# Slots and banks given out by the longest free time, and gathered rows transposed as fp32r

## The chip, the cores and the metric

The kernel runs on one core of one Trainium2 chip. The metric is the device time of one execution in microseconds (us); lower is better. The core has five engines that run side by side: TensorE (PE in the views, PEld for its weight loads), VectorE (DVE), ScalarE (ACT), GpSimd (POOL) and SyncE (SP), which here only issues DMAs. Each engine takes its own instructions in the order in which they stand in the program; engines wait for one another, and for DMAs, on semaphores.

## What is computed

Two decoder layers over 512 tokens of width 1024, in float32. Each layer mixes the tokens with two kinds of attention, normalizes, sends every token to 2 of 16 experts, and normalizes again. Cut to what matters here:

```python
def reference(x, w_in, ..., exp_w_gate, exp_w_up, exp_w_down, ln2_g, ln2_b):
    for l in range(DEPTH):                                   # DEPTH = 2
        mix = token_mixer(x, w_in[l], ...)                   # sparse and stick-breaking attention
        x = layer_norm(DN_ALPHA * x + mix, ln1_g[l], ln1_b[l])
        ffn = grouped_moe(x, w_router, router_bias, exp_w_gate[l], exp_w_up[l], exp_w_down[l])
        x = layer_norm(DN_ALPHA * x + ffn, ln2_g[l], ln2_b[l])
    return x

def grouped_moe(...):
    # scores, the best group of 4 experts, the 2 best experts in it, weights that sum to 1
    for e in range(N_EXPERTS):                               # 16 experts, D_EXPERT = 512
        h = jax.nn.silu(xf @ exp_w_gate[e]) * (xf @ exp_w_up[e])
        y = y + combine[:, e:e + 1] * (h @ exp_w_down[e])
```

## The kernel before

**Products.** A float32 product is made of three products of a faster type, fp32r (float32 bits, read in a reduced way): each operand is split into a high part (a cast, on ScalarE) and a low part (the difference, on VectorE), and TensorE adds low by high, high by low and high by high into one PSUM bank (`mm3`). So every weight tile that arrives by DMA (512 KB, one slot) goes through one ScalarE cast and one VectorE subtraction, and each of the two writes a slot of its own before TensorE reads it.

**The recorder and its plan.** The kernel body doesn't issue instructions; it records operations on named buffers. A planner in Python (`Recorder.plan`) then walks through them with an estimated duration for each, orders them on every engine, and gives every buffer a place: one of 48 SBUF slots `s` of 4 KB in each of the 128 partitions, of 56 small ones `m`, of 8 `t` or the one `k`, or one of 4 PSUM banks `p` and 4 banks `a`. `room` says when enough places are free for an operation, `take` picks which ones. At run time a buffer in a place waits, through semaphores, until the last reader of the buffer that had the place before is done; this is the only thing that the choice of a place can alter at run time. In the views a tile is named by its place, so `s` stands for any of the 48 slots, `p` and `a` for banks; `ident` is the identity matrix for transposes, `x1d` and `zd` are arrays in DRAM.

**Loads.** All weights and inputs are loaded by SyncE (line 526), one DMA after another in the planned order, each into a slot from the same 48. A load waits at the head of this queue until its slot is free.

**One expert.** `moe` runs over the 16 experts. For experts 1 to 15 `gather` (line 1179, GpSimd) fetches up to 128 token rows from `x1d` by an index list into a slot `xg`; `transpose_tile` turns it by 8 transposes of 128x128 on TensorE (line 445) into a bank `a`, and the split into high and low parts follows. Expert 0 takes its rows from two banks that a product with one-hot rows filled. Then come gate, up and down products (line 447), and 4 more transposes of the hidden activations (`turn` in `down`). `add_rows` (line 1184, GpSimd) adds the result rows into `zd` by an indirect DMA, called scatter-add below; it reads its slot until it has landed. The last expert's rows are added on TensorE instead. Its up product runs in two halves of 256 columns.

**The overflow block.** An expert that gets more than 128 rows is finished by `overflow` (lines 1199 to 1234), a branch on all engines behind the gather of the last expert's work. For these inputs the branch is not taken. Its buffers, five slots `s` among them, are taken from the planner like others and count as free again after it. At run time the skipped branch still brings up the semaphores that its DMAs would have brought up, on GpSimd's queue (names that begin with DMASW; DMAHW are SyncE's queue).

**Closing LayerNorm.** The rows of `zd` are loaded back into slots, multiplied by the identity into banks `p` (`p<-s,ident`) together with the last expert's rows, and normalized on VectorE and ScalarE.

The lines of `take` that set the choice before: `s.sort()` orders the free places of a kind by the time at which they became free, and the index is the largest whose time is not after now.

Of the kernel before, what the change touches and what calls it, by code (L numbers as in the profile page):

```python
# [11 lines left out]
F = mybir.dt.float32  # L12
FR = mybir.dt.float32r
# [9 lines left out]
P = 128  # L23
S = 512
D = 1024
# [28 lines left out]
class View:  # L54
# [19 lines left out]
    def real(self):  # L74
        x = self.buf.tile
        for f, a, k in self.chain:
            x = getattr(x, f)(*a, **k)
        return x
# [13 lines left out]
class Recorder:  # L92
# [82 lines left out]
    def plan(self):  # L175
# [93 lines left out]
        def take(o, t):  # L269
            for b in o.allocs:  # L270
                s = slots[b.kind]
                s.sort()
                i = max((j for j in range(len(s)) if s[j][0] <= t + 1e-9), default=0)
                b.slot = s.pop(i)[1]
                g = b.group
                if g is not None:
                    if live[g] >= self.QUOTA[g]:
                        heapq.heappop(glive[g])
                        live[g] -= 1
                    live[g] += 1  # L280
                    turn[g].pop()
# [3 lines left out]
        while done < len(self.ops):  # L285
            best = None
            for e in engs:
# [3 lines left out]
                t = free[e] if ready[e] else (pend[e][0][0] if pend[e] else None)  # L291
                if t is not None and (best is None or t < best[0]):
                    best = (t, e)
            if barrier and not any(p.prio < barrier[0].prio for e in engs for p in [x[3] for x in pend[e]] + [x[2] for x in ready[e]] if p.prio < barrier[0].prio):
                o = barrier.pop()
                t = max([o.ready] + [free[x] for x in engs if x != "SP"])
# [3 lines left out]
                t = w  # L300
                e = "ALL"
            else:
                if best is None:
                    self.explain(blocked, slots, live)
                t, e = best
# [3 lines left out]
                o = None  # L309
                if e == "ACT" and table is not None:  # L310
                    keep = [x for x in ready[e] if x[2].table in (None, table)]
                    if keep:
                        x = min(keep)
                        if x[0] < ready[e][0][0] + 400:
                            ready[e].remove(x)
                            heapq.heapify(ready[e])
                            o = x[2]
                if o is None:
                    o = heapq.heappop(ready[e])[2]
# [100 lines left out]
class Chip:  # L420
# [13 lines left out]
    def mm(self, out, terms, start, stop, transpose=None, also=()):  # L434
        dt = {F: 4, FR: 1, BF: 1}
        n = self.n(out)
        if transpose is not None:
            dur = 0.11
        else:
            dur = sum(max(dt[x.dtype if not isinstance(x, View) else x.ap.dtype] * n, 256) / 2400 + 0.004 for _, x in terms)  # L440

        def fn():
            o = real(out)
            if transpose is not None:
                self.nc.tensor.transpose(o, real(transpose[0]), transpose[1])  # L445
            for i, (w, x) in enumerate(terms):
                self.nc.tensor.matmul(o, real(w), real(x), start=start and i == 0, stop=stop and i == len(terms) - 1)  # L447
        reads = [x for t in terms for x in t] + ([transpose[0]] if transpose else [])
        o = self.r.add("PE", dur, fn, [out], reads, allocs=also)
        o.cols = sum(n * w.shape[0] / P for w, _ in terms) + n * (transpose is not None)  # L450
        o.cnt = sum(2 if (x.ap.dtype if isinstance(x, View) else x.dtype) == F else 1 for _, x in terms) + (transpose is not None)
        return o
# [91 lines left out]
def build(tc, x0, xT0, w_idx, w_main, w_br, w_out, w_exp, bgate, idxg, idxb,  # L544
          ln1g, ln1b, ln2g, ln2b, wrt, rbias, ln1c, hconst, tab0, out):
    nc = tc.nc
    with ExitStack() as ctx:
# [17 lines left out]
        C = Chip(R)  # L565


        ident = const.tile([P, P], F, name="ident")
        make_identity(nc, ident)
        identb = const.tile([P, P], BF, name="identb")  # L570
        nc.vector.tensor_copy(identb, ident)
        jp = const.tile([P, P], I32, name="jp")
# [28 lines left out]
        def s4(shape, dtype=F, group=None, reserve=0):  # L601
            return R.buf("s", shape, dtype, group, reserve)
# [10 lines left out]
        wr = const.tile([P, KD, NE], F, name="wr")  # L613
        rb = const.tile([P, NE], F, name="rb")
        lnc = const.tile([P, DEPTH, 2, KD], F, name="lnc")
        onesf = const.tile([P, P], F, name="onesf")
        nc.vector.memset(onesf, 1.0)
        loaded = []
        bias_t = const.tile([P, 256 + 384 + 512], BF, name="bias")
# [56 lines left out]
            for n in range(2):  # L676
                C.stt(dst[:, half(n)], dst[:, half(n)], rstd, b[:, half(n)], OP.mult, OP.add)

        def transpose_tile(src, dst_of):
            for hb in range(2):  # L680
                ps = bank("a")
                for k in range(4):
                    c = (hb * 4 + k) * P
                    C.tr(ps[:, k * P:(k + 1) * P], src[:, c:c + P], ident)
                dst_of(hb, ps)

        def proj_tok(l, xT, c, done, before=None):
# [489 lines left out]
        def gather(dst, idx, also, skip):  # L1177
            kw = dict(bounds_check=S - 1, oob_is_err=False) if skip else {}
            R.add("POOL", 1.04, lambda: nc.gpsimd.indirect_dma_start(  # L1179
                out=real(dst), out_offset=None, in_=x1d, in_offset=IOA(ap=real(idx), axis=0), **kw),  # L1180
                [dst], [idx], rtok=[f"x1{t}" for t in range(NT)], nbytes=P * (2048 if skip else 4096), allocs=also)
# [58 lines left out]
        def moe(l, tb, gl, mci, loads, xacc, until, routed):  # L1240
            def prep(e):
                xh, xl = s4([P, KD, P], FR, "xh"), s4([P, KD, P], FR, "xh")

                def dst(hb, ps):
                    ks = slice(hb * 4, hb * 4 + 4)
                    C.split(xh[:, ks, :], xl[:, ks, :], ps.rearrange("p (k t) -> p k t", k=4))
                if e == 0:
                    xg = s4([P, D], group="xg")
                    C.copy(xg[:, half(0)], xacc[0])
                    C.v("tensor_copy", xg[:, half(1)], xacc[1])  # L1250
                    transpose_tile(xg, dst)
                    return xh, xl
                xg = s4([P, D], group="xg")
                last = e == NE - 1
                gather(xg, gl[:, 0:1] if last else tb[:, e, 0:1], [xh, xl], not last)
                transpose_tile(xg, dst)
                return xh, xl

            def weights(e, i):
# [330 lines left out]
```

## Time and profile before

| | |
|---|---|
| median of 3 runs | 1536.97 us (1535.93 to 1539.32) |
| the profiled execution | 1539.54 us |
| its span (first to last instruction) | 1537.7 us |
| TensorE, VectorE, ScalarE busy | 1475.2, 1249.5, 896.6 us |
| granted TensorE clock, mean | 0.983 |
| moved by DMA | 308.52 MB, mean 201 GB/s |

The span falls into attention of layer 0 (to about 360 us), merge, first LayerNorm and router (to about 460), experts (to about 747) and the second LayerNorm, and the same for layer 1, which ends with the output.

How to read the lines below. A line of the timeline has the start, the length, engine, source line, operation, tiles written and read, shape and count of a run of like instructions, and in brackets the idle time before it with what ended it. A line of the waits has who waited for whom: total, times and the longest. A line of the stretches has the stretch, its length, busy time of PE, PEld, DVE, ACT and POOL, the granted clock, the DMA engines' share and GB/s. A group has its count, its busy time, the mean ns of one, and the idle time before. Matmuls overlap: the mean ns of one includes its latency, and the rate is read from many in a row.

### The profile page before, as it was taken

Reading aid. Unit: us, or ns where it says so; the run is one execution under the profiler, and the core shown is the slowest. Engines: PE = TensorE matmul, PEld = TensorE weight load, DVE = VectorE, ACT = ScalarE, POOL = GpSimd, SP = SyncE. Lnnn points to the kernel's source line nnn. Section 1 sums busy time; section 2 is a strip of 40 time slices with the busy share of each in tenths; the row PEclk is TensorE's granted clock in tenths of the full one; section 3 lists DMA queues with packets and bytes.
Section 4 is the critical chain, followed back from the end, with each engine's and each line's share of the span. In section 5 each row is a group of like instructions: output and inputs, shape, how many; then the busy total and the mean of one; then the engine's idle time right before and its main releaser. Section 6 shows DMA issues by size and latency. Waiting matters only on the chain. (4 is left out here: it accounts for less than half of the span.)

```text
span 1537.7 us, 21018 instructions
## 1 busy us (share of the span) xinstructions
PE 1475.2 (96%) x7188; PEld 1178.9 (77%) x7188; DVE 1249.5 (81%) x2301; ACT 896.6 (58%) x1459; POOL 142.4 (9%) x127
## 2 busy tenths in 40 slices
PE   8999999999989999999799999999999899999985
PEld 7877777777867878888588777777778578888874
DVE  5699996777587989999765999867766789999975
ACT  4335543675146878888623455446831478888873
POOL 0000000000031131210010000000001212112110
PEclk9999999999999999999999999999999899999998
DMA  6221112117888989999712221221287889999962
GB/s 217 71 91 57 68 56 89 63 42 288 302 280 297 337 309 348 341 334 333 237 61 69 83 61 50 82 83 55 70 306 279 302 307 351 341 352 339 351 216 108
DMA packets 91265, 308.52 MB, mean 201 GB/s; under 512 B 15439, under 2 KB 15567, under 8 KB 91152
## 3 DMA queue, kind: packets, MB, share of 16 engines
q1 hardware_dynamic: 82000, 290.69, 53.5%
q0 software_dynamic: 9152, 16.43, 4.5%
q8 instruction: 58, 0.95, 0.2%
q14 instruction: 55, 0.45, 0.1%
HBM read 293.80 MB, written 28.46 MB: 210 GB/s over the span
## 5 line engine op out<-in xcount | busy, mean ns | idle before, releaser
L447 PE MATMUL p<-s,s 128*128 128x512 f32 (+1 forms) x5192 | 1268.1, 398 | 28.1 <-DVE s L495 25.7
L447 PEld LDWEIGHTS p<-s,s 128*128 128x128 f32 x5192 | 952.9, 191 | 234.9 <-DVE s L495 25.5
L495 DVE TENSOR_TENSOR s<-s,s 128x1024 fp32r<-128x1024 f32 (+2 forms) x526 | 612.1, 1195 | 152.4 <-ACT s L484 112.3
L484 ACT CAST s<-s 128x1024 fp32r<-128x1024 f32 (+2 forms) x526 | 518.2, 1029 | 226.6 <-PE p L447 141.6
L495 DVE TENSOR_TENSOR s<-a,s 128x256 fp32r<-128x256 f32 (+3 forms) x386 | 169.5, 479 | 36.5 <-ACT s L484 32.7
L484 ACT CAST s<-a 128x256 fp32r<-128x256 f32 (+2 forms) x354 | 127.1, 414 | 109.8 <-PE a L445 103.7
L445 PE MATMUL a<-ident,s 128*128 128x128 f32 x888 | 134.0, 277 | 13.5 <-DMA s<-x1d,m 6.4
L445 PEld LDWEIGHTS a<-ident,s 128*128 128x128 f32 x888 | 106.7, 142 | 44.9 <-issue 11.5
L523 POOL TENSOR_TENSOR m<-m,nhalf 128x1 f32<-128x1 f32 x24 | 17.8, 741 | 891.0 <-DVE m L495 881.6
L480 ACT ACTIVATE s<-a 128x512 f32<-128x512 f32 (+3 forms) x156 | 61.9, 450 | 46.0 <-PE a L447 27.5
L484 ACT COPY s<-a 64x512 f32<-64x512 f32 (+1 forms) x48 | 27.8, 583 | 96.7 <-PE a L445 45.3
L1184 POOL DMA_INDIRECT zd<-s,m x30 | 61.1, 2035 | 199.8 <-ACT s L487 167.4
L487 ACT ACTIVATE s<-p,m 128x512 f32<-128x512 f32 (+1 forms) x64 | 44.1, 689 | 53.5 <-PE p L447 50.6
L1179 POOL DMA_INDIRECT s<-x1d,m x30 | 43.6, 1452 | 267.9 <-PE p L447 220.2
L464 PE MATMUL a<-s,s 64*128 64x384 f32 (+3 forms) x456 | 67.4, 351 | 0.0
L447 PEld LDWEIGHTS a<-s,s 128*128 128x128 f32 x360 | 57.0, 188 | 9.2 <-issue 2.2
L447 PE MATMUL a<-s,s 128*128 128x324 f32 (+4 forms) x360 | 62.2, 321 | 1.5 <-DVE s L495 1.3
L464 PEld LDWEIGHTS a<-s,s 64*128 64x128 f32 x456 | 41.3, 185 | 27.6 <-issue 20.4
L495 DVE MAX8 m<-s 128x8 f32<-128x256 f32 (+2 forms) x96 | 53.4, 556 | 1.8
L495 DVE MATCH_REPLACE8 s<-m,s 128x256 f32<-128x256 f32 (+2 forms) x96 | 52.0, 542 | 0.0
L495 DVE TENSOR_TENSOR_SCAN s<-s 128x128 f32<-128x128 f32 (+3 forms) x64 | 51.0, 812 | 0.1
L484 ACT CAST s<-p 128x512 fp32r<-128x512 f32 x48 | 27.9, 588 | 38.5 <-DVE p L495 22.7
(107 smaller groups left out, 632.4 us busy)
## 6 DMA issues: line engine op xcount, KB each, us to landing
s<-in_w_exp SPq DMA_DIRECT2D x384, 512.0 KB
s<-in_w_main SPq DMA_DIRECT2D x79, 512.0 KB
s<-in_w_br SPq DMA_DIRECT2D x16, 512.0 KB
s<-in_w_out SPq DMA_DIRECT2D x16, 512.0 KB
x1d<-s SPq DMA_DIRECT2D x8, 512.0 KB
zd<-s SPq DMA_DIRECT2D x8, 512.0 KB
s<-zd SPq DMA_DIRECT2D x8, 512.0 KB
s<-in_w_idx SPq DMA_DIRECT2D x8, 324.0 KB
```

Of the source, the lines that this page charges most:

```text
L445: self.nc.tensor.transpose(o, real(transpose[0]), transpose[1])
L447: self.nc.tensor.matmul(o, real(w), real(x), start=start and i == 0, stop=stop and i == len(terms) - 1)
L464: self.nc.tensor.matmul(real(o), real(t[i][0]), real(t[i][1]), start=i == 0, stop=stop and i == len(t) - 1)
L480: self.nc.scalar.activation(real(out), real(src), func, bias=real(bias), scale=real(scale), **kw)
L484: return self.r.add("ACT", 0.1 + self.psum(out, src) + self.n(out) * 0.833e-3, lambda: self.nc.scalar.copy(real(out), real(src)), [out], [ ...
L487: return self.r.add("ACT", 0.2 + self.n(out) * 0.833e-3, lambda: self.nc.scalar.mul(real(out), real(src), real(c)), [out], [src, c])
L495: getattr(self.nc.vector, method)(real(out), *[real(a) for a in args], **{k: real(x) for k, x in kw.items()}, **({} if accum is None else ...
L523: return self.r.add("POOL", 0.47, lambda: self.nc.gpsimd.tensor_tensor(real(out), real(a), e, OP.pow), [out], [a])
L1179: R.add("POOL", 1.04, lambda: nc.gpsimd.indirect_dma_start(out=real(dst), out_offset=None, in_=x1d, in_offset=IOA(ap=real(idx), axis=0), * ...
L1184: rows = R.add("POOL", 1.04, lambda: nc.gpsimd.indirect_dma_start(out=zd, out_offset=IOA(ap=real(idx), axis=0), in_=real(src), in_offset=None,
```

## The change

Two edits. In `take`, the place is no longer the one freed last but, for every kind except `m`, index 0 of the sorted list: the one that has been free longest. And the gathered rows are held and transposed as fp32r: `xg` is an fp32r tile (the gather writes it through a float32 view), `transpose_tile` gets the matrix to transpose by as an argument, and the output bank is viewed in that matrix's type. The identity is now an fp32r tile `identr`, copied by VectorE from a float32 one at the start; the other transposes read it through a float32 view. The float32 identity is built in the tile `onesf`, which is set to ones afterwards.

```diff
@@ take @@
-                i = max((j for j in range(len(s)) if s[j][0] <= t + 1e-9), default=0)
+                i = max((j for j in range(len(s)) if s[j][0] <= t + 1e-9), default=0) if b.kind == "m" else 0
@@ tr @@
-                self.nc.tensor.transpose(o, real(transpose[0]), transpose[1])
+                self.nc.tensor.transpose(o.bitcast(transpose[1].dtype), real(transpose[0]), transpose[1])
@@ constants @@
-        ident = const.tile([P, P], F, name="ident")
-        make_identity(nc, ident)
+        onesf = const.tile([P, P], F, name="onesf")
+        make_identity(nc, onesf)
+        identr = const.tile([P, P], FR, name="identr")
+        nc.vector.tensor_copy(identr, onesf)
+        ident = identr.bitcast(F)
...
-        onesf = const.tile([P, P], F, name="onesf")
         nc.vector.memset(onesf, 1.0)
@@ transpose_tile @@
-        def transpose_tile(src, dst_of):
+        def transpose_tile(src, dst_of, by=ident):
...
-                    C.tr(ps[:, k * P:(k + 1) * P], src[:, c:c + P], ident)
+                    C.tr(ps[:, k * P:(k + 1) * P], src[:, c:c + P], by)
@@ prep, experts 1 to 15 @@
-                xg = s4([P, D], group="xg")
+                xg = s4([P, D], FR, group="xg")
...
-                gather(xg, gl[:, 0:1] if last else tb[:, e, 0:1], [xh, xl], not last)
-                transpose_tile(xg, dst)
+                gather(xg.bitcast(F), gl[:, 0:1] if last else tb[:, e, 0:1], [xh, xl], not last)
+                transpose_tile(xg, dst, identr)
```

The number of free places at any time does not depend on which is picked, so the order of the operations stays nearly the same; what changes nearly everywhere is the slot numbers and with them the waits. Below, a name like s45_14898 is slot 45 and the buffer's number; the brackets list the semaphores that the instruction waits on.

VectorE behind the overflow block of layer 1, in the last expert: the low parts of its last weights (128x1024), and the product's other half taken up (128x256). Before:

```order
L495 TENSOR_TENSOR s25_14889<-s47_14572,s31_14766 128x1024 [waits DMAHW3_49,Activation_49]
L495 TENSOR_TENSOR s45_14898<-s16_14589,s35_14891 128x1024 [waits DMASW0_49,DVE_49,DMAHW4_49,PE_49,Activation_49]
L495 TENSOR_TENSOR s27_14912<-s43_14603,s33_14896 128x1024 [waits DMAHW5_49,PE_49,Activation_49]
L495 TENSOR_TENSOR s43_14930<-s22_14618,s16_14917 128x1024 [waits DMASW1_49,DMAHW6_49,DVE_49,Activation_49]
L495 TENSOR_TENSOR s42_14907<-s42_14907,p1_14900 128x256 [waits PE_49]
```

Now:

```order
L495 TENSOR_TENSOR s47_14890<-s20_14573,s38_14767 128x1024 [waits DMAHW3_49,DVE_49,Activation_49]
L495 TENSOR_TENSOR s11_14899<-s2_14590,s4_14892 128x1024 [waits DMAHW4_49,PE_49,Activation_49]
L495 TENSOR_TENSOR s17_14913<-s30_14604,s13_14897 128x1024 [waits DMAHW5_49,PE_49,Activation_49]
L495 TENSOR_TENSOR s15_14931<-s8_14619,s5_14918 128x1024 [waits DMAHW6_49,PE_49,Activation_49]
L495 TENSOR_TENSOR s16_14908<-s16_14908,p1_14901 128x256 [waits PE_49]
```

No row moved; the second and fourth had slots of the overflow block (s45, whose weights the block would load) or tied to GpSimd's queue, and now have not.

The same place in layer 0. Before:

```order
L495 TENSOR_TENSOR s44_7401<-s25_7107,s41_7393 128x1024 [waits DMASW4_49,DMAHW6_49,PE_49,Activation_49]
L495 TENSOR_TENSOR s43_7417<-s2_7232,s45_7399 128x648 [waits DMASW7_49,DMASW3_49,DMAHW5_49,DVE_49,Activation_49]
L495 TENSOR_TENSOR s35_7432<-s47_7127,s10_7415 128x1024 [waits DMASW3_49,DMAHW7_49,PE_49,Activation_49]
L495 TENSOR_TENSOR s46_7407<-s46_7407,p3_7403 128x256 [waits PE_49]
L495 TENSOR_TENSOR s42_7454<-s0_7234,s25_7428 128x648 [waits DMAHW6_49,Activation_49]
```

Now:

```order
L495 TENSOR_TENSOR s33_7398<-s29_7112,s22_7390 128x1024 [waits DMAHW5_49,PE_49,Activation_49]
L495 TENSOR_TENSOR s1_7412<-s39_7125,s36_7396 128x1024 [waits DVE_49,DMAHW6_49,PE_49,Activation_49]
L495 TENSOR_TENSOR s3_7427<-s43_7136,s20_7417 128x1024 [waits DVE_49,DMAHW7_49,PE_49,Activation_49]
L495 TENSOR_TENSOR s5_7407<-s5_7407,p1_7400 128x256 [waits PE_49]
L495 TENSOR_TENSOR s26_7449<-s46_7256,s4_7425 128x648 [waits DMAHW5_49,Activation_49]
```

A weight split of the next layer (128x648, second row before) moved behind one of the last expert's; the three waits on GpSimd's semaphores are gone from these rows.

ScalarE in layer 0, among the first experts, 12 rows behind the last one that writes s23_5337, which a scatter-add then reads; weights are cast to their high parts. Before:

```order
L484 CAST s47_5447<-s31_4884 128x1024 [waits DMASW7_49,DMASW5_49]
L484 CAST s44_5456<-s43_4899 128x1024 [waits DMASW3_49,DVE_49]
L484 CAST s2_5465<-s25_4912 128x1024 [waits PE_49]
L484 CAST s23_5477<-s29_4929 128x1024 [waits DMASW2_49]
L484 CAST s4_5484<-s26_5155 128x1024 [waits DMAHW3_49,DVE_49,PE_49]
```

Now the same scatter-add reads s34_5332, and its slot goes to VectorE's row in the middle here, the low part of the weight before that of s29_4929:

```order
L495 TENSOR_TENSOR s30_5460<-s37_4899,s28_5446 128x1024 [waits Activation_49]
L495 TENSOR_TENSOR s1_5472<-s42_4911,s43_5454 128x1024 [waits DMASW3_49,DVE_49,Activation_49]
L495 TENSOR_TENSOR s34_5485<-s7_4925,s12_5464 128x1024 [waits DMASW2_49,Activation_49]
L495 TENSOR_TENSOR s23_5414<-s23_5414,p1_5431 128x512 [waits PE_49]
L495 TENSOR_TENSOR s4_5504<-s47_4955,s33_5474 128x1024 [waits Activation_49]
```

So the wait for the scatter-add moved from ScalarE to VectorE, and one weight forward.

## The prediction

> **What bounds the kernel now.** I read the page first (its busy times, the slices and the granted clock), then the waits of TensorE, then the stretches, and last the timeline at each place where TensorE stood still.
>
> ```profile
> PE 1475.2 (96%) x7188; PEld 1178.9 (77%) x7188; DVE 1249.5 (81%) x2301; ACT 896.6 (58%) x1459; POOL 142.4 (9%) x127
> ...
> PEclk9999999999999999999999999999999899999998
> ...
> zd<-s,m POOLq DMA_INDIRECT x30, 9.2
> ```
> ```profile
> PE p L447 <- DVE s L495: 28.2, 15, 6.7
> PE a L445 <- DMA s<-x1d,m: 6.4, 5, 2.6
> ```
> ```profile
> 40.00:360.00 320.00, 318.77 (x1629) 249.61 (x1629) 263.18 (x628) 164.07 (x362) 1.96 (x3) 1.00 0.21 69
> ...
> 480.00:720.00 240.00, 236.72 (x1107) 195.51 (x1106) 217.10 (x212) 197.15 (x237) 45.40 (x25) 0.99 0.98 340
> ```
>
> TensorE is the bound: 1475.2 of 1537.7 us. In the attention stretch of layer 0 it is busy 318.77 of 320 us, so slot numbers there have nothing to hide or to give. Its waits on VectorE add up to 28.2 us in 15 waits; these are few and large, and the change can reach only some. In the experts' stretch TensorE is busy 236.72 of 240 us beside a DMA share of 0.98: two resources nearly full at once.
>
> **The transposes.** Each expert from 1 to 15 transposes 8 blocks of gathered rows, in one run with 4 blocks of the hidden activations:
>
> ```profile
> 603.57 1.47 PE L445 MATMUL a<-ident,s 128*128 128x128 f32 x12
> 604.80 16.62 PE L447 MATMUL p<-s,s 128*128 128x512 f32 x72
> 621.26 1.47 PE L445 MATMUL a<-ident,s 128*128 128x128 f32 x12
> ```
> ```profile
> 752.68 1.88 PE L447 MATMUL p<-s,ident 128*128 128x512 f32 x4
> ```
> ```profile
> L447 PE MATMUL p<-s,ident 128*128 128x512 f32 x24 | 11.4, 596 | 2.5 <-DVE s L495 2.5
> ```
>
> The 12 transposes occupy 1.47 us; less the last one's latency of 0.27 they start every 0.109 us. The fp32r products (72 in 16.62 us, the last 0.39) start every 0.229 us for 512 columns, a quarter of which is 0.057. The plain f32 products by the identity (4 in 1.88 us, the last 0.59) start every 0.43 us, a quarter of which is 0.107. So a transposing of 128 f32 columns costs what plain f32 costs, and fp32r streams at nearly twice the rate. The kernel already runs 64 fp32r products of 128 columns, in pairs behind a pair of 256 columns:
>
> ```profile
> 134.77 0.57 PE L447 MATMUL a<-s,s 128*128 128x256 f32 x4
> 135.19 0.29 PE L445 MATMUL a<-ident,s 128*128 128x128 f32 x1
> ```
> ```profile
> L447 PE MATMUL a<-s,s 128*128 128x256 f32 x2 | 0.4, 283 | 0.0
> L447 PE MATMUL a<-s,s 128*128 128x128 f32 x2 | 0.3, 248 | 0.0
> ```
>
> The four start within 0.42 us of the next instruction; two halves of 0.229 leave 0.19, or 0.095 for each of 128 columns, the step to another kind included. Upper end: 240 transposes (30 experts by 8) by (0.109 - 0.06) = 11.8 us. With 0.095 it would be 3.4. Lower end: 0, if something else sets the 0.109. I take 10, near the upper end because 0.107 meets 0.109 so closely that streaming must set it, and less than it because the first two gathers of a layer are waited for anyway (6.4 us above). The other 648 transposes keep f32.
>
> The Trainium skill, "TensorE: Matmul & The Clock Gate", section "LDWEIGHTS (loading the stationary operand)", gives a weight load P/1.2 ns, with P the columns; an estimate from it is 107 ns for 128 columns. By that rule the weight loads would set the 0.109 us, fp32r would save nothing, and the sum below would be 10 us smaller. The row of 0.109 agrees with it; the pairs of 128 columns, at 0.095 or less, speak against it.
>
> **The ends of the layers.** After the last gate products stands the overflow block, a branch that is not taken here. Its SBUF tiles count as freed at that moment, so "freed last" hands them to the next weight splits; VectorE then waits on the GpSimd queue's DMA semaphores, which come up only behind the last scatter-add.
>
> ```profile
> 1490.92 2.18 POOL L1184 DMA_INDIRECT zd<-s,m  x1 [7.12 <-ACT s L484]
> ```
> ```profile
> 1498.12 3.68 DVE L495 TENSOR_TENSOR s<-s,s 128x1024 fp32r<-128x1024 f32 x3 [6.45 <-DMA zd<-s,m]
> ```
> ```profile
> 1499.40 3.36 PE L447 MATMUL p<-s,s 128*128 128x256 f32 x14 [5.12 <-DVE s L495]
> 1503.27 2.12 PE L447 MATMUL p<-s,s 128*128 128x256 f32 x15 [0.51 <-DVE s L495]
> ...
> 1512.47 1.88 PE L447 MATMUL p<-s,ident 128*128 128x512 f32 x4
> ```
> ```profile
> 741.33 3.48 PE L447 MATMUL p<-s,s 128*128 128x256 f32 x18 [3.87 <-DVE s L495]
> ...
> 760.60 1.98 PE L447 MATMUL p<-s,ident 128*128 128x512 f32 x4 [2.46 <-DVE s L495]
> ```
> ```profile
> 739.72 1.23 DVE L495 TENSOR_TENSOR s<-s,s 128x1024 fp32r<-128x1024 f32 x1 [3.15 <-DMA zd<-s,m]
> ```
> ```profile
> 740.00:750.00 10.00, 7.29 (x35) 6.12 (x36) 9.31 (x12) 5.59 (x8) 0.00 (x0) 0.83 0.79 268
> ...
> 1490.00:1510.00 20.00, 13.11 (x74) 11.37 (x73) 8.91 (x11) 6.12 (x8) 2.18 (x1) 0.83 0.33 102
> ```
>
> In the changed order the same splits of VectorE name only hardware-queue, TensorE, ScalarE or VectorE semaphores; one ScalarE cast at each end still names a GpSimd one, of a scatter two uses of its slot earlier, a whole expert back. Layer 1: the idle 5.12 us goes, and with it part of the reduced clock behind it (14 products in 3.36 us against 15 in 2.12; 0.83 granted): about 1.3 us more. What is late next is the reload of the scattered rows for the closing LayerNorm: its queue also waits for the last scatter, which lands near 1498, while that LayerNorm's first product runs at 1512.47, or about 1506 afterwards; 8 us are left, enough for four loads. So this end is worth 6 of at most 6.9 (5.12 + 0.51 + 1.3), and nothing hides it: it is the program's tail. Layer 0: TensorE idles 3.87, VectorE 3.15, and the LayerNorm that follows waits for VectorE (2.46 at 760.60). What carries through is therefore VectorE's 3.15; I take 3 (ends 0 and 5.2, which is 3.87 and 1.3 of clock).
>
> **Slots that a scatter-add still reads.** Two stalls in the experts:
>
> ```profile
> 557.30 0.50 PE L447 MATMUL p<-s,s 128*128 128x512 f32 x1 [1.81 <-ACT s L484]
> 558.56 7.73 PE L447 MATMUL p<-s,s 128*128 128x512 f32 x20 [0.76 <-DVE s L495]
> ```
> ```profile
> 556.21 2.94 ACT L484 CAST s<-s 128x1024 fp32r<-128x1024 f32 x3 [6.64 <-DMA zd<-s,m]
> ```
> ```profile
> 540.28 7.45 POOL L1184 DMA_INDIRECT zd<-s,m  x1 [5.03 <-ACT s L487]
> ```
> ```profile
> 540.00:580.00 40.00, 37.43 (x164) 30.37 (x163) 32.46 (x33) 28.63 (x36) 12.06 (x4) 0.91 0.90 310
> ```
> ```profile
> 1258.27 5.89 PE L447 MATMUL p<-s,s 128*128 128x512 f32 x23 [1.91 <-DVE s L495]
> ```
>
> At 557 a cast wants the slot whose scatter-add was issued at 540.28 and held GpSimd for 7.45 us, where others take about 2. It costs 2.57 us of idle time and some 3 more of clock (a granted 0.91 over 40 us is 3.6 us, part of it inside the idle time). The changed order does not free this place: the slot of the same scatter goes to VectorE's split of the weight one before, so the wait stands a little earlier. If that scatter is as late again, the stall stays or grows by 1; if it is not, neither kernel shows it. Ends -1 and +5.6; I take 1. At 1258 the split's new slot has no scatter behind it: 1.91, all of it.
>
> **The rest.** The banks: at 366.72 and 1126.65 TensorE waits 1.82 us for the first of four banks, all in use, before and after; no gain.
>
> ```profile
> 366.72 3.48 PE L447 MATMUL p<-s,s 128*128 128x512 f32 x14 [1.82 <-DVE s L495]
> ```
>
> The loads are queued in the same order. In attention they may run further ahead, which no engine waits for; in the experts the queue is at 0.98. The extra copy of the identity is one 128x128 VectorE copy, like this one, and the first product comes 5 us later behind input loads:
>
> ```profile
> 1.46 0.25 DVE L571 CAST identb<-ident 128x128 bf16<-128x128 f32 x1 [1.46 <-POOL ident masks.py:199]
> ```
>
> Its bounds are 0 and 0.25; I take 0. TensorE's instructions that wait grow by about 250 in number; those satisfied long before cost nothing visible (the 72 products above keep 0.229 with such waits among them). I allow -2 for those that are not, and for the loads: an expert's 12 loads of 0.524 MB take 18.5 us at 340 GB/s against TensorE's period of 17.69 (603.57 to 621.26), so the lead gained in attention shrinks, and faster by 0.39 it shrinks more, 14 times: at worst 5.5 us a layer.
>
> ```profile
> s<-in_w_exp SPq DMA_DIRECT2D x384, 512.0 KB
> ```
> ```profile
> ACT s L484 <- DMA s<-in_w_idx: 2.2, 1, 2.2
> ```
>
> The second row is the only wait for a load among ScalarE's waits from 480 to 740 us, and it is not for an expert's. At the start of layer 1 some VectorE rows and one load change places; VectorE sets the pace there in both orders, so I take 0, with 2 either way.
>
> Sum: 10 + 6 + 3 + 1 + 1.9 - 2 = 20 us. The profiled execution took 1539.5 (span 1537.7 and 1.8 around it), which is 2.6 above the median of 1537.0; the sum would make it 1519.5, and 1517 of the median.
>
> **The rivals.** First, the loads become the bound: share 0.98 speaks for it, that no cast waits for an expert's load speaks against. It takes up to 11 of the 11.8 and leaves the stalls (6 + 3 + 1 + 1.9, less 1 for waits): 1537 - 11 = 1526. Second, fp32r transposes are no faster (half of the change does nothing): 1537 - 20 + 10 = 1527; the quarter of an fp32r product, 57 ns, speaks against. Third, slower: "longest free" in a pool that the experts keep almost empty returns the slots of scatter-adds a set distance behind each scatter, and VectorE or ScalarE then stops in every expert as at 557. One such stop costs up to 5.6 us; it decides from four more stops (22 us), and six would give 1537 - 20 + 34 = 1551. For it speaks that a scatter takes 9.2 us to land and that the changed split at 557 waits earlier; against it, that the slots' distance does not shrink elsewhere. Fourth, both halves cancel against new waits: 1537.
>
> **How the numbers follow.** Forecast 0.6, loads 0.11, no gain from fp32r 0.14, slower 0.09, no change 0.06. A measurement tells about 0.2%, 3 us. Faster 0.85, same 0.06, slower 0.09. The forecast's own range is 1506 (11.8 + 6.9 + 5.2 + 5.6 + 1.9 = 31.4) to 1525; taking in the two rivals of 1526 and 1527, with a profile's noise on them, the range is 1506 to 1529.
>
> **What would show it.** Right: runs of transposes per expert of about 1.1 us for 12, a period near 17.3; no wait of VectorE on scatters around 736 and 1492 and no idle TensorE of 4 to 5 us there; the stall at 1258 gone. Wrong: 1.47 us for 12 as now; casts that wait for expert loads near the end of a layer; waits on scatters in many experts with clock drops behind them.

## The result, and the profile after

| | before | after |
|---|---|---|
| median, runs side by side | 1538.14 us (1535.93 to 1541.99, 4 runs) | 1513.52 us (1512.39 to 1515.85, 4 runs) |
| ratio | | 0.9839, interval 0.9815 to 0.9863 |
| span of the profiled execution | 1537.7 us | 1511.4 us |
| TensorE busy | 1475.2 us | 1460.1 us |

The change makes the kernel 24.6 us faster, 1.6%. Measured once more in a later group it took 17.8 us off (0.9885, interval 0.9863 to 0.9907; experiment 4). What makes the two gains differ by 6.8 us is not known. All medians and ratios leave out two executions far slower than the rest, of 8018 us (`fr_only`) and 2081 us (the kernel before, experiment 5).

The page of the profile after, its first busy line, and then the longest waits of TensorE (who waits for whom, total, times, longest):

```profile
PE 1460.1 (97%) x7188; PEld 1168.7 (77%) x7188; DVE 1242.7 (82%) x2302; ACT 890.7 (59%) x1459; POOL 141.4 (9%) x127
```
```profile
PE p L447 <- DVE s L495: 20.4, 13, 6.7
PE a L445 <- DMA s<-x1d,m: 7.7, 4, 5.2
```

Waits on VectorE fell from 28.2 to 20.4 us; the wait for gathered rows grew from 6.4 to 7.7.

The timeline of TensorE after, at one expert in the steady run of layer 0, at the end of layer 0, and at the end of layer 1 (the views write f32 for fp32r too; the name `identr` marks the new identity, which the f32 transposes of other tiles read as well):

```profile
592.95 1.23 PE L445 MATMUL a<-identr,s 128*128 128x128 f32 x12
594.01 16.59 PE L447 MATMUL p<-s,s 128*128 128x512 f32 x72
610.44 1.23 PE L445 MATMUL a<-identr,s 128*128 128x128 f32 x12
...
707.20 0.60 PE L445 MATMUL a<-identr,s 128*128 128x128 f32 x4
...
725.96 2.42 PE L447 MATMUL p<-s,s 128*128 128x256 f32 x18 [0.51 <-DVE s L495]
...
736.35 1.88 PE L447 MATMUL p<-s,identr 128*128 128x512 f32 x4
...
746.78 3.78 PE L447 MATMUL p<-s,identr 128*128 128x512 f32 x4 [4.96 <-DVE s L495]
750.35 1.28 PE L445 MATMUL a<-identr,s 128*128 128x128 f32 x8
```
```profile
1458.70 12.54 PE L447 MATMUL p<-s,s 128*128 128x512 f32 x54
...
1477.48 2.06 PE L447 MATMUL p<-s,s 128*128 128x256 f32 x15 [0.52 <-DVE s L495]
...
1486.43 1.88 PE L447 MATMUL p<-s,identr 128*128 128x512 f32 x4
```

An expert's period is 610.44 - 592.95 = 17.49 us, 0.20 less than the 17.69 before. At the layer ends the idle 3.87 us are down to 0.51 and the 5.12 are gone. But the LayerNorm behind layer 0 now stands still for 4.96 us where it stood for 2.46. The same marks in the timeline of before:

```profile
719.22 0.60 PE L445 MATMUL a<-ident,s 128*128 128x128 f32 x4
...
762.42 1.04 PE L445 MATMUL a<-ident,s 128*128 128x128 f32 x8
...
1477.71 12.54 PE L447 MATMUL p<-s,s 128*128 128x512 f32 x54
```

From the last expert's 4 transposes to the LayerNorm's first product by the identity (752.68 and 1512.47 before) the end of layer 0 takes 29.15 us instead of 33.46, 4.3 less, and from its 54 products on the end of layer 1 takes 27.73 instead of 34.76, 7.0 less. From that first product to the first 8 transposes the LayerNorm behind layer 0 takes 14.0 instead of 9.7: 4.3 more.

### The profile page after: what moved, and what is told of

Same layout as the page of the kernel before. It is cut to its first block, busy times and chain, and to the rows that moved or that the text cites. A ratio compares the mean times of both kernels' runs of the same rounds, so it can differ in the third digit from the quotient of the medians.

```text
span 1511.4 us, 20936 instructions
## 1 busy us (share of the span) xinstructions
PE 1460.1 (97%) x7188; PEld 1168.7 (77%) x7188; DVE 1242.7 (82%) x2302; ACT 890.7 (59%) x1459; POOL 141.4 (9%) x127
## 5 line engine op out<-in xcount | busy, mean ns | idle before, releaser
L495 DVE TENSOR_TENSOR s<-s,s 128x1024 fp32r<-128x1024 f32 (+1 forms) x526 | 606.8, 1192 | 84.6 <-ACT s L484 72.0
L484 ACT CAST s<-s 128x1024 fp32r<-128x1024 f32 (+1 forms) x526 | 515.6, 1033 | 67.7 <-PE p L447 28.2
L445 PE MATMUL a<-identr,s 128*128 128x128 f32 x888 | 125.0, 271 | 14.3 <-DMA s<-x1d,m 7.7
L445 PEld LDWEIGHTS a<-identr,s 128*128 128x128 f32 x888 | 102.5, 142 | 44.6 <-issue 15.5
L523 POOL TENSOR_TENSOR m<-m,nhalf 128x1 f32<-128x1 f32 x24 | 17.8, 743 | 877.8 <-DVE m L495 509.5
L1186 POOL DMA_INDIRECT zd<-s,m x30 | 56.0, 1868 | 254.5 <-ACT s L487 205.2
L1181 POOL DMA_INDIRECT s<-x1d,m x30 | 47.5, 1583 | 203.3 <-PE p L447 103.1
```

The lines of the kernel that those rows point to most:

```text
L445: self.nc.tensor.transpose(o.bitcast(transpose[1].dtype), real(transpose[0]), transpose[1])
L484: return self.r.add("ACT", 0.1 + self.psum(out, src) + self.n(out) * 0.833e-3, lambda: self.nc.scalar.copy(real(out), real(src)), [out], [ ...
L495: getattr(self.nc.vector, method)(real(out), *[real(a) for a in args], **{k: real(x) for k, x in kw.items()}, **({} if accum is None else ...
L523: return self.r.add("POOL", 0.47, lambda: self.nc.gpsimd.tensor_tensor(real(out), real(a), e, OP.pow), [out], [a])
L1181: R.add("POOL", 1.04, lambda: nc.gpsimd.indirect_dma_start(out=real(dst), out_offset=None, in_=x1d, in_offset=IOA(ap=real(idx), axis=0), * ...
L1186: rows = R.add("POOL", 1.04, lambda: nc.gpsimd.indirect_dma_start(out=zd, out_offset=IOA(ap=real(idx), axis=0), in_=real(src), in_offset=None,
```

## The experiments

Ten kernels ran, two of them twice, in three groups; each group shares runs of the kernel before on its chip. "New order" is the choice of the place free longest, "old order" that of the place freed last.

### 1. Each half of the change alone

`fr_only` has the fp32r transposes under the old order (all of the diff but its first line); `lru_only` has the new order with the f32 transposes:

```diff
@@ take, lru_only @@
-                i = max((j for j in range(len(s)) if s[j][0] <= t + 1e-9), default=0)
+                i = max((j for j in range(len(s)) if s[j][0] <= t + 1e-9), default=0) if b.kind == "m" else 0
```

> Only the fp32r transposes; places are again given out by the time freed last. Theory: 8 of the 12 transposes of an expert start every 0.084 instead of 0.109 us, 0.2 us an expert, so 240 of them are worth 5 to 6 us and no more; the idle TensorE behind the overflow block (about 4 and 5 us) stays, and VectorE's waits on scatter-adds there with it. About 1532 against 1538. Rival, that the two halves help only together: no difference from the kernel before, within 2 us.

> Only the choice of the place freed longest; transposes in f32 as before. Theory: the changed kernel's gain of 24 us less the 5 to 6 of the transposes, about 18 to 19, so 1519; the waits behind the overflow block are gone in both layers. Rival, that the time went with a slow scatter-add that only the profiled run of the kernel before had: 10 to 12 us of gain, about 1527.

Before 1535.14. `fr_only` 1531.7, ratio 0.9986 (0.9962 to 1.001): inconclusive, between 6 us faster and 2 slower. `lru_only` 1511.82, 23.3 us faster, 0.9847 (0.9818 to 0.9876). So the new order alone gives what the whole change gives, better than the 18 to 19 that I expected, and the fp32r transposes nothing that these runs show. Yet they save TensorE time: `fr_only` has the period of 17.49 too, `lru_only` that of 17.69 (593.64 to 611.33).

```profile
593.64 1.47 PE L445 MATMUL a<-ident,s 128*128 128x128 f32 x12
594.87 16.62 PE L447 MATMUL p<-s,s 128*128 128x512 f32 x72
```

### 2. What in the new order does it: overflow slots, all slots, banks

`mru_spare` keeps the old order, but takes a slot of the skipped overflow block only when no other is free; `lru_s` has the new order for the slots `s` alone, `lru_banks` for the banks `p` and `a` alone.

```diff
@@ take, mru_spare @@
+                if (b.kind, s[i][1]) in spare:
+                    i = max((j for j in range(len(s)) if s[j][0] <= t + 1e-9 and (b.kind, s[j][1]) not in spare), default=i)
+                spare.discard((b.kind, s[i][1]))
@@ plan, where a buffer's place becomes free @@
+                    if o.eng == "ALL" and b.kind == "s":
+                        spare.add((b.kind, b.slot))
@@ take, lru_s and lru_banks: the end of the line, one each @@
+ ... if b.kind != "s" else 0
+ ... if b.kind not in "pa" else 0
```

> The kernel before with one rule more: places are given out by the time freed last, but SBUF slots that the overflow block held are taken only when no other slot is free. Theory: the two waits behind the block were due to these slots alone, so both go: 7 us at the end of layer 1 and 3 to 4 at the end of layer 0, of which the LayerNorm after may take some back; 1528 to 1531. Rival, that the waits there come from any slot tied to a scatter-add: the idle 4 and 5 us stay, 1537 to 1538.

> The place freed longest for SBUF slots alone; PSUM banks by the time freed last; transposes in f32. Theory: the banks do nothing, since TensorE's waits for banks stood where all four were in use, so the time is that of the run with both, within 2 us. Rival: banks freed long ago spare TensorE short waits in every stretch, and 4 us or more of the gain are missing here.

> The kernel before with the new order for the PSUM banks alone; the slots in SBUF still go to the one freed last. Theory (slots carry the change, banks take 1 to 5 us, the difference of the new order for both and for slots alone, 4.8 us between medians and 2 between profiles): 1 to 5 us below the kernel before, and the waits of 3.9 and 5.1 us at the two layer ends stay. Rival (banks alone are worth nothing, they only help once the slots are spread): within 1 us of the kernel before.

| | median | ratio |
|---|---|---|
| `mru_spare` | 1526.41 (before 1535.14) | 0.9936 (0.9913 to 0.996) |
| `lru_s` | 1516.64 (before 1535.14) | 0.9874 (0.9841 to 0.9907) |
| `lru_banks` | 1533.15 (before 1534.7) | 1.0004 (0.998 to 1.0027) |

Timelines of TensorE at the layer ends: `mru_spare` (lines are 6 higher), then `lru_banks`.

```profile
736.00 2.42 PE L453 MATMUL p<-s,s 128*128 128x256 f32 x18 [1.16 <-DVE s L501]
...
1470.69 18.25 PE L453 MATMUL p<-s,s 128*128 128x512 f32 x93
1489.45 2.06 PE L453 MATMUL p<-s,s 128*128 128x256 f32 x15 [0.51 <-DVE s L501]
```
```profile
732.27 4.21 PE L447 MATMUL p<-s,s 128*128 128x256 f32 x18 [4.60 <-DVE s L495]
...
1486.48 3.36 PE L447 MATMUL p<-s,s 128*128 128x256 f32 x14 [5.33 <-DVE s L495]
```

Keeping the overflow block's slots out of the way takes away 2.7 of the 3.87 us at the end of layer 0 and all 5.12 at the end of layer 1, where TensorE runs on without that gap (the 0.51 at 1489.45 was there before too); it is worth 8.7 us, about what was expected. The mechanism in the prediction is shown by this: the slots of a branch that isn't taken carry the semaphores of GpSimd's queue.

The new order for all slots is worth 18.5, so 9.8 more than keeping the overflow block's slots away. That is clear of the noise (every run of `mru_spare` lies above every run of `lru_s`), but where it comes from stays open. The two profiles differ by 7.8 us: 2.8 before the experts of layer 0, 4.1 in those experts, where `mru_spare` has a late scatter-add (experiment 3), and some 1 behind; the first two also differ between profiles of one order.

The banks alone show nothing, between 3 us faster and 4 slower, and the end stalls stay with them, as expected. Slots and banks together (`lru_only`) are 4.8 below slots alone, and all five runs (1510.95 to 1515.06) lie below all four of `lru_s` (1515.66 to 1517.2), so the expectation that the banks do nothing failed. Why they help only beside the new order of slots is not shown; TensorE's waits on VectorE's results are 18.5 us in the profile of `lru_s` and 16.2 in that of `lru_only`.

### 3. The scatter-add that held GpSimd

The prediction called the 557 us stall a thing of one late scatter-add. The timelines of GpSimd, at that instruction: after, `mru_spare`, and a later kernel, `half_lru`, one expert earlier.

```profile
536.20 1.79 POOL L1186 DMA_INDIRECT zd<-s,m  x1 [6.08 <-ACT s L487]
```
```profile
539.44 7.45 POOL L1190 DMA_INDIRECT zd<-s,m  x1 [5.03 <-ACT s L493]
```
```profile
521.65 7.99 POOL L1187 DMA_INDIRECT zd<-s,m  x1 [6.46 <-DMA s<-in_w_exp]
```

And TensorE before, from one run of transposes to the next around it:

```profile
544.45 1.47 PE L445 MATMUL a<-ident,s 128*128 128x128 f32 x12
...
568.20 1.47 PE L445 MATMUL a<-ident,s 128*128 128x128 f32 x12
```

The transposes are 23.75 us apart instead of 17.69: the late scatter-add cost the profiled execution before 6.1 us. It is not an accident of one execution: it came again in `mru_spare` at the same instruction and with the same 7.45 us, and in `half_lru`, which has the new order, where TensorE then waits 4.22 us. It did not come in the other eleven profiles. What sets it off, and how often it comes in executions without a profile, stays open. The scatter of the times doesn't settle it: the 20 runs of the kernel before span 15.1 us and the 5 of `lru_only` 4.1, but the 5 of `half_lru`, with the new order, span 11.0.

### 4. Where the transposes' time went, first place: the LayerNorm behind layer 0

Profile after, in the order SyncE's wait, the stretches around it (stretch, length, busy time of PE, PEld, DVE, ACT, POOL, clock, DMA share, GB/s), SyncE's issues and ScalarE:

```profile
SPq L1492 <- DMA zd<-s,m: 16.7, 1, 16.7
```
```profile
715.00:722.00 7.00, 6.85 (x32) 5.42 (x31) 6.40 (x6) 6.53 (x8) 0.04 (x1) 1.00 0.26 69
722.00:729.00 7.00, 6.09 (x49) 5.64 (x48) 6.46 (x8) 5.91 (x8) 2.10 (x1) 1.00 0.08 12
```
```profile
728.01 0.57 SPq L1492 DMA_DIRECT2D tabd<-in_tab  x1
...
731.24 4.49 SPq L526 DMA_DIRECT2D s<-in_w_main  x6
```
```profile
739.97 1.05 ACT L484 CAST s<-s 128x1024 fp32r<-128x1024 f32 x1 [2.73 <-DMA s<-in_w_main]
...
743.46 0.59 ACT L480 ACTIVATE s<-p 128x512 f32<-128x512 f32 x1
```

SyncE stands 16.7 us at a small copy of a table (64 KB, from one DRAM array to another), which waits for the last scatter-add, while the DMA engines are nearly idle (0.26 and 0.08). The weights for layer 1 queue behind it, and the first lands at about 740. ScalarE has three casts of these weights ahead of the LayerNorm's first sums (743.46), so the LayerNorm waits for a load that it doesn't need, and a TensorE that comes earlier only waits longer. The 24 products ahead of the LayerNorm and the stall in it, in `lru_only`:

```profile
732.86 7.35 PE L447 MATMUL p<-s,s 128*128 128x512 f32 x24 [0.97 <-DVE s L495]
...
747.79 3.62 PE L447 MATMUL p<-s,ident 128*128 128x512 f32 x4 [2.28 <-DVE s L495]
```

There the products took 7.35 us and the stall 2.28; after, they took 5.74 (the same 24 at full rate) and the stall 4.96. `after_ln` and `lru_ln` make these casts wait for tile 0 of the LayerNorm instead:

```diff
@@ ln2 @@
-                    C.stt(r[:, c], r[:, c], rstd, lb[:, c], OP.mult, OP.add)
+                    o = C.stt(r[:, c], r[:, c], rstd, lb[:, c], OP.mult, OP.add)
+                if t == 0:
+                    normed[l] = o
@@ vb_by_tile @@
-                w += split_w(load_w(w_main[l, M_VB, k2 // 2], 2 * (k2 % 2)), group="wo")
+                w += split_w(load_w(w_main[l, M_VB, k2 // 2], 2 * (k2 % 2)), group="wo", after=normed[l - 1])
```

> The whole change once more, beside the kernels of this group, to settle what the fp32r transposes are worth under the new slot order (the new order alone took 23.3 us off its kernel before; the whole change took 24.6 in another group). Theory (the 6 us that TensorE saves are taken back by a longer LayerNorm behind layer 0 and by a longer wait for the first gather of layer 1): 23 to 26 us below the kernel before, no more than 2 below the new order alone. Rival (the two groups only ran on different chips, and the 5 us are there): 27 to 30 us below.

> The whole change, and in layer 1 the four casts of the weights for the indexer's V product wait until the last step of tile 0 of the LayerNorm behind layer 0, so that ScalarE and VectorE don't stand at a load that lands at 740 us while the LayerNorm could run. Theory (the LayerNorm's stall of 4.96 us comes from engines that stand in order behind a late load): the stall falls to 0 to 2.5 us, the transposes behind it start 2.5 to 4 us earlier, and the kernel is 2 to 4 us faster than the whole change. Rival (the load itself is the bound there, and TensorE then waits for the same weights a few us later, or at the first gather of layer 1): same time within 1 us.

> The new slot and bank order with the f32 transposes of the kernel before, and the same wait of the four casts for the LayerNorm as in after_ln. Its stall there was 2.28 us, so theory: 0 to 2 us faster than the new order alone (which was 23.3 below the kernel before), and so 3 to 5 us slower than after_ln: with the LayerNorm out of the loads' way the transposes' 5 to 6 us show in the time. Rival (TensorE time saved in the expert stages is worth nothing, the loads pace it): within 1 us of after_ln.

Before 1534.7. `after_again` 1516.95 (ratio 0.9885, 0.9863 to 0.9907), a gain of 17.8 where the two expectations were 23 to 26 and 27 to 30: both missed. `after_ln` 1511.38 (0.9856, 0.983 to 0.9883), `lru_ln` 1512.19 (0.985, 0.9826 to 0.9874). The timeline of TensorE in `after_ln`:

```profile
741.16 1.50 PE L447 MATMUL p<-s,s 128*128 128x512 f32 x4
742.49 1.88 PE L447 MATMUL p<-s,identr 128*128 128x512 f32 x4
744.21 1.04 PE L445 MATMUL a<-identr,s 128*128 128x128 f32 x8
```

The stall is gone, so its cause is shown. `after_ln` is 5.6 us below the whole change beside it, more than the 2 to 4 expected, though the intervals touch. But `lru_ln` is only 0.8 above `after_ln`: the last expectation, that the transposes' time would now show, failed. With the f32 transposes the dependency shows no gain: `lru_ln` is 22.5 below its kernel before, `lru_only` was 23.3 below its own.

### 5. Second place: is TensorE time worth anything here?

The two kernels ran again beside two that leave out half of the gathered rows' transposes (the splits read the first bank twice), under each order. That also alters the result of layer 0, and with it perhaps the rows that layer 1 gathers; what this does to the time was not separated.

```diff
@@ transpose_tile, half_lru (on lru_ln) and half_mru (on before) @@
             for hb in range(2):
+                if half and hb:
+                    dst_of(hb, ps)
+                    continue
                 ps = bank("a")
```

> lru_ln with half of the gathered rows' transposes left out (of the 8 blocks of 128 columns only 4 are transposed, and the splits behind them read those 4 twice): 120 transposes at 0.109 us, 13 us less on TensorE, with the planner's costs and everything else as in lru_ln. It asks what TensorE time is worth under the new order at all. Theory 1 (the loads pace the expert stages: in lru_ln their DMA share is 0.99 to 1.00 from 480 to 700 us at 353 to 365 GB/s, and 12 loads of 512 KB by 17.7 us need 356): 0 to 5 us below lru_ln. Theory 2 (TensorE paces them, as its 99 to 100% busy share there says): 10 to 14 us below lru_ln.

> The kernel before with the same half of the transposes left out, 13 us less on TensorE. fp32r transposes alone, 6 us less on TensorE, had moved it by 2 us (interval 6 down to 2 up). Theory 1 (loads held back by slots pace it): 0 to 5 us below the kernel before. Theory 2 (TensorE's time counts in full, and the 2 us were the 6 seen through runs that scatter over 15 us): 10 to 14 us below the kernel before.

> after_ln once more, beside lru_ln and half_lru on one chip. Theory 1 (loads pace): within 2 us of lru_ln. Theory 2 (TensorE paces): 4 to 6 us below lru_ln, as their two profiles read (spans 1507.2 and 1512.8).

> lru_ln once more, the mark for the three others: 1510 to 1514 us.

| | median (before 1536.67) | ratio |
|---|---|---|
| `lru_ln_b` | 1508.61 | 0.9821 (0.9802 to 0.984) |
| `after_ln_b` | 1509.22 | 0.9823 (0.98 to 0.9846) |
| `half_lru` | 1506.61 | 0.9797 (0.9777 to 0.9818) |
| `half_mru` | 1522.47 | 0.9909 (0.9886 to 0.9932) |

Under the old order 13 us of TensorE time less are worth 14.2 us: theory 2. Some of it may be the late scatter-add, which the profile of the kernel before has and that of `half_mru` hasn't. Under the new order they are worth 2.0 against `lru_ln_b`, with overlapping intervals: theory 1. And `after_ln_b` equals `lru_ln_b` a second time, within 0.6; `lru_ln_b` came out a little below the 1510 to 1514 expected. But theory 1's reason, that the loads pace the experts, does not hold in the steady part. One expert's transposes to the next, TensorE in `half_lru`:

```profile
602.07 1.03 PE L445 MATMUL a<-ident,s 128*128 128x128 f32 x8
...
619.28 1.03 PE L445 MATMUL a<-ident,s 128*128 128x128 f32 x8
```

The period falls to 17.21 us and TensorE doesn't wait; the DMA engines follow. The time is lost at single places where TensorE, being earlier, meets a DMA that isn't. In `half_lru` these are the late scatter-add of experiment 3 and the first gathers of layer 1:

```profile
539.36 0.80 PE L447 MATMUL p<-s,s 128*128 128x512 f32 x1 [4.22 <-ACT s L484]
```
```profile
1210.59 1.09 PE L445 MATMUL a<-ident,s 128*128 128x128 f32 x4 [3.10 <-DMA s<-x1d,m]
...
1232.90 0.30 PE L445 MATMUL a<-ident,s 128*128 128x128 f32 x1 [3.07 <-DMA s<-x1d,m]
```

This profile is the slowest execution of `half_lru` (1512.69, median 1506.61). The expert with the late scatter-add takes 24.50 us in it (525.93 to 550.43) instead of 17.21; whether the median contains that loss is not known.

For the fp32r transposes the pair `after_ln_b` and `lru_ln_b` shows the second place; GpSimd's first gather of layer 1 and TensorE behind it, then both kernels' steady part and end, first `after_ln_b`:

```profile
1195.12 1.34 POOL L1181 DMA_INDIRECT s<-x1d,m  x1 [8.55 <-PE p L447]
```
```profile
1205.27 2.10 PE L445 MATMUL a<-identr,s 128*128 128x128 f32 x12 [6.27 <-DMA s<-x1d,m]
...
1305.22 1.23 PE L445 MATMUL a<-identr,s 128*128 128x128 f32 x12
...
1473.57 2.06 PE L447 MATMUL p<-s,s 128*128 128x256 f32 x15 [0.52 <-DVE s L495]
```

and `lru_ln_b`:

```profile
1197.21 1.34 POOL L1179 DMA_INDIRECT s<-x1d,m  x1 [7.49 <-PE p L447]
```
```profile
1204.24 1.50 PE L445 MATMUL a<-ident,s 128*128 128x128 f32 x12 [2.08 <-DMA s<-x1d,m]
...
1302.85 1.47 PE L445 MATMUL a<-ident,s 128*128 128x128 f32 x12
...
1473.00 2.05 PE L447 MATMUL p<-s,s 128*128 128x256 f32 x15 [0.51 <-DVE s L495]
```

The kernel with fp32r issues its gather 2.1 us earlier and has its rows 1.0 us later: 10.2 us from issue to use against 7.0. A lead of 2.1 becomes a lag of 1.0. In the first experts of layer 1 it loses 1.3 more, though each should give 0.2 (100.0 against 98.6 us from the first gathered rows to the run at 1305.22 or 1302.85), and the last ten experts win most of it back: at the end of layer 1, 1473.57 and 1473.00, they stand 0.6 apart. The other profiles of the new order agree in most: from the issue of this gather to its use it takes 9.2, 7.0 and 8.9 us with fp32r (`after`, `after_again`, `after_ln`) and 6.8, 6.6 and 7.1 with f32 (`lru_only`, `lru_s`, `lru_ln`). Why the gather is slower in three of the four isn't shown; other loads are in flight around it in both kernels, issued in the same order, but nothing was run that takes them away.

## Why the prediction was right, and where not

The predicted 1517 for a median of 1537 was a gain of 20; 24.6 were measured, 17.8 in the second group, inside the range of 1506 to 1529. The terms did not come out so evenly:

| step of the prediction | forecast | what the runs showed |
|---|---|---|
| fp32r transposes | 10 | about 6 on TensorE; in the time nothing shown under the new order, at most 6 under the old |
| end of layer 1 | 6 | 7.0, all kept |
| end of layer 0 | 3 | 4.3, given back by the LayerNorm |
| stall at 557 | 1 | 6.1 in the profiles, the late scatter-add not coming |
| stall at 1258 | 1.9 | gone; new waits of 0.47 at 1262 and 0.75 at 1281 |
| new waits and loads | -2 | 2.2 more at the first gathers of layer 1 (19.55 instead of 17.35 from the 48 products ahead of them to the products behind) |
| start of layer 1 | 0 | the LayerNorm 4.3 longer, its stall 4.96 instead of 2.46; a wait of 1.33 behind it gone |

**The transposes** are the step that failed. Their price was taken as 0.06 us from a quarter of a 512-column product; the signs set for it were 1.1 us for 12 and a period of 17.3. Measured were 1.23 and 17.49: with 8 of the 12 in fp32r, the 0.20 less put each of them 0.025 below the 0.109, at 0.084. That is 6 us for 240. The other end I had, 0.095 from the pairs of 128 columns, was the nearer row and should have had more weight than a quarter of a longer instruction. And the argument for the upper end, that 0.107 of plain f32 meets the 0.109, rests on a misread row. The LayerNorms have 16 products by the identity (2 layers, 4 tiles of 128 tokens, 2 halves each), and the profile before counts 32, the 24 that the prediction shows and 8 more:

```profile
L447 PE MATMUL a<-s,ident 128*128 128x512 f32 x8 | 3.8, 592 | 0.0
```

So one plain f32 product is two records of 0.43 us. Its quarter is 0.215 and not 0.107; an f32 transpose, one record of 0.109, doesn't cost what plain f32 costs, and nothing said that it would gain what a product gains.

The Trainium skill, "TensorE: Matmul & The Clock Gate", section "LDWEIGHTS (loading the stationary operand)", gives a weight load 107 ns (an estimate from its P/1.2). Had such a load set the spacing, as the prediction read it, there would have been no gain on TensorE at all; the spacing of 0.084 speaks against that reading. The rival "no gain from fp32r" was thus right on what this half is worth under the new order and wrong on the cause. The rival "the loads become the bound" holds only at single places. The prediction summed TensorE's savings over 30 experts as if nothing stood behind them; the kernels with half of the transposes agree with this sum under the old order (14.2 for 13) and not under the new (2.0 for 13).

**The ends** were right in mechanism and size, at layer 1 for the whole and at layer 0 for the place; `mru_spare` shows the cause. What the prediction missed is what is late next at layer 0: it named the reload of scattered rows at layer 1, but not, at layer 0, the load for which SyncE's queue stands.

**The stall at 557** was put down at 1 because the same wait stays, moved to VectorE; that was right on the wait (`half_lru`, with the new order and a scatter-add that is late, has a stall again), and the gain in the trace comes from the scatter-add not being late.

**Luck.** That the sum landed near the result is partly luck: 4 us too much for the transposes and the LayerNorm's 4.3 stand against the 5 too little at 557. The table also doesn't hold the whole difference. Its steps in the traces come to 18.9 us (6 + 7.0 + 4.3 + 6.1 + 0.7 - 2.2 - 4.3 + 1.3; 0.7 is 1.91 less the two new waits), and the two profiles lie 26.3 apart. Of the rest, 3.1 are there before the first experts: the same 4 transposes start at 457.45 us after and 460.56 before, and between 457.35 and 462.19 in the fourteen profiles of all kernels. Another 1.7 lie in layer 1, where 144 products take 34.59 us before and 32.94 after; they take 34.56 in `lru_ln` and 32.94 or 32.95 in all others. These two differ between executions of either order, so the change can't claim them. A further 1.5 lie at 6 products of layer 1's merge (4.94 and 3.42; 4.93 in `lru_only`), and 1.1 stay unplaced.

**The slower rival**, waits on scatter-adds in many experts, did not come: in the steady experts after, TensorE is busy for 239.59 of 240 us (236.72 before).

```profile
480.00:720.00 240.00, 239.59 (x1147) 199.22 (x1145) 221.38 (x222) 203.65 (x247) 41.51 (x25) 1.00 0.98 354
```

The best complete kernels are `lru_ln` and `after_ln`, each twice: 0.985 and 0.9821, 0.9856 and 0.9823, some 22 to 28 us below the kernel before. The fp32r transposes can be left out of them at no loss that these runs show.

## What to carry to other kernels

Hand out buffers by the longest free time where a planner reuses them, above all buffers of a branch that may be skipped: the semaphores of a skipped branch come up late, and whoever takes its slot at once waits for them. A saving on the busiest engine is worth its sum only as long as nothing stands at the next joint; read each joint (first gather, first load of the next stage, a load queue that stands at a small transfer) and ask what arrives there at a fixed time. On in-order engines keep work on late loads behind work that is ready: that one dependency took away a stall of 5 us, though a gain in time showed only with the fp32r transposes.

## What was not expected of the hardware

The same program's profiled executions differ at the same wait. Both lines are TensorE behind the wait of 1.8 us at the start of the merge, in the profiles of the whole change, first and second:

```profile
365.40 14.80 PE L447 MATMUL p<-s,s 128*128 128x512 f32 x64 [1.81 <-DVE s L495]
```
```profile
366.68 13.70 PE L447 MATMUL p<-s,s 128*128 128x512 f32 x52 [1.82 <-DVE s L495]
```

Once 64 products run in 14.80 us, 0.23 each; once 52 take 13.70, which is 1.7 us more than 52 at that rate, with a granted clock of 1.00 and 0.96 in the stretch from 360 to 400 us. Seven of the fourteen profiles show the slower form here (0.26 to 0.27 each), and two at the 144 products behind the like wait in layer 1. So one wait costs its own length and, in some executions, about as much again at a lower clock. A difference of 2 us between two single profiles shows nothing by itself here.
